# 8-KB slots for all expert weights, with four of them shared in turn with the mixer's normalized input

## The chip, the cores and the metric

The kernel runs on one core of one Trainium2 chip. The metric is the device time of one execution in microseconds (us). The kernel before was timed in three runs: 1904.22, 1905.45 and 1908.49 us, median 1905.45 us. Differences under about 0.2% (3.8 us) can't be told from no change.

## The reference, cut to what matters

Two decoder layers over 512 tokens of 1024 numbers, all in float32. Each layer has a mixer and a mixture of experts (MoE):

```python
for l in range(2):
    sh1, sc1, g1, sh2, sc2, g2 = split(silu(c) @ ada_w[l] + ada_b[l])
    h = rmsnorm(x, norm1_g[l]) * (1 + sc1) + sh1
    x = x + g1 * hybrid_mixer(h, w_in[l], ...)      # three kinds of attention, one output projection
    h = rmsnorm(x, norm2_g[l]) * (1 + sc2) + sh2
    x = x + g2 * hier_moe(h, ...)                   # top 1 of 4 groups, top 2 of 8 experts in it
return rmsnorm(x, final_g)

# one expert:  (silu(xc @ w1[e]) * (xc @ w3[e])) @ w2[e],  w1, w3: 1024x512, w2: 512x1024
```

A layer has 32 experts. Each has 4 MB of first weights (w1 and w3) and 2 MB of second weights (w2), so a layer reads 192 MB of expert weights, once.

## The kernel before, in words

**Mixer.** `ln1` normalizes x, transposes it and keeps it as `h`: eight 4-KB tiles (high and low part of a 128-row block; sizes here are per partition, of which there are 128). `proj_qk` and `proj_v` multiply `h` with the input projection's weights; the last of them is the second half of `proj_qk(1)` ("q1" in the list `ORDER`). After it nothing reads `h`. `ORDER` is written out by hand and interleaves attention units (`sb`, `fox`, `nsa`), projections, conditioning vectors (`ada`), output projection (`p..`, `w..`) and the four `tail` sequences, each of which ends the mixer for 128 tokens and starts their routing: `moe_in` transposes x into `xT` for the router and `moe_parts` writes the normalized rows to DRAM (`rows`, line 1173, issued by ACT).

**MoE.** `route` ranks tokens per expert. `gather` (line 1355, issued by POOL) fetches the rows of two experts at a time by an indirect DMA into `XR`, `turn` transposes them into `xeT`, `up(e)` multiplies with w1 and w3 (line 1380), `act(e)` forms the hidden values, `down(e)` multiplies with w2 (line 1410), `down_out` splits the product into a high and a low part `Yh`, `Yl`, and once for each two experts `scatter` (line 1442) multiplies with a selection matrix and adds to x (line 454). In the source the order is up(e), down(e-1), act(e), scatter for even e.

**Loads.** All weights come by DMAs that SP issues (line 227) in the order of the list `todo`. `pump` gives the next load a free slot. There are two kinds of slots. 8-KB slots (1 MB over 128 partitions): 3 of the `ring`, which lives through the whole kernel and also serves the mixer's weights, 6 (`r0` to `r5`) in the MoE's pool, 2 (`t0`, `t1`) used once at the MoE's start; they hold first weights, four loads an expert. 4-KB slots (512 KB): `s0`, `u0` and eight tiles of the pool tag `L`, of which six stay in use; they hold second weights, four loads an expert. `L` has 18 tiles of 4 KB, which the mixer uses for `h`, the split queries and keys, the values and the output projection's inputs, and the MoE for `xr`, `xeT`, `G`, `Yh` and `Yl`. At the MoE's start `early` issues 18 loads in the order of `FREED`. The pools of mixer and MoE lie over the same memory, so `r`, `t`, `s` and `u` slots are free only when the mixer's tiles under them have been read for the last time.

**Order.** The framework in which the kernel is written orders the instructions of each engine when the kernel is built: an instruction is placed when its inputs and its tile are there by the framework's own account of durations, the earlier one in the source first. The engines then run that order as it stands and wait by semaphores. `keep_in_program_order` pins a few instructions. So the order of `up`, `down` and `scatter` on PE can differ from the source.

Of the kernel before, what the change touches and what calls it, by code (L numbers as in the profile page):

```python
# [10 lines left out]
F32 = mybir.dt.float32  # L11
# [77 lines left out]


RING, RING2, RINGT = 3, 6, 2
BIG = "ring", "r", "t"

FREED = "s0 r0 r2 r1 L L L L r5 t0 t1 u0 r4 r3 L L l l"

PT_K = 0, 1024, 1792, 2304
PT_W = 2560
BUFS = {"L": 18, "v": 1, "W": 8, "P": 4, "o": 6, "us": 4}
ROT = [i ^ 8 if i < 16 else i for i in range(32)]


# [12 lines left out]
class K:  # L114
# [63 lines left out]
    def plan(self):  # L178
        a, t = self.a, self.todo
        for l in self.layers:  # L180
            for s in dict.fromkeys(self.loads(l)):
                if s[0] == "ada":
                    m, nm, c = s[1:4]
                    col = MOD[nm] * 1024 + c * 512
                    for h in range(2):
                        t.append((("ada", m, nm, c, h), a["ada_w"][m, col // 512, h], [128, 4, 512]))
                elif s[0] == "qk":
                    t.append((("wqk", l, s[1]), a["wqk"][l, s[1]], [128, 2, NK, 128]))
                elif s[0] == "v":
                    t.append((("wv", l, s[1]), a["wv"][l, s[1]], [128, NK, 256]))  # L190
                elif s[0] == "cmp":
                    for kv in "kv":
                        t.append((("cmp", l, kv), a["cmp_w1_" + kv][l], [128, 16, 128]))
                elif s[0] == "prep" or s == ("tail", 0):
                    ks = s[1] if s[0] == "prep" else (3,)
                    src = a["w_out"][l, 128 * ks[0]:128 * ks[-1] + 128, :].rearrange("(j p) n -> p j n", p=128)
                    t.append((("wo", l, ks), src, [128, len(ks), D]))
            if self.moe_on:

                for e in range(NE + 1):  # L200
                    for h in range(4 if e < NE else 0):
                        t.append((("w13", l, e, h), a["expert_w13"][l, e, h], [128, 2, 2, 512]))
                    for h in range(4 if e else 0):
                        t.append((("w2", l, e - 1, h), a["expert_w2"][l, e - 1, 128 * h:128 * h + 128, :], [128, D]))

    def pump(self):
        full = set()
        for x in list(self.todo):
            key, src, shape = x
            own = key[0] in ("w13", "w2") and key[1] == self.layer  # L210

            if self.limit and not own or len(full) == 2:
                return
            big = key[0] != "w2"
            slot = next((p for p in self.free if (p.rstrip("0123456789") in BIG) == big and (p == "ring" or own)), None)
            if slot is None:
                full.add(big)
                continue
            if big in full:
                continue  # L220
            self.todo.remove(x)
            self.free.remove(slot)
            self.load(slot, key, src, shape)

    def load(self, slot, key, src, shape):
        x = self.slot(slot, shape, "ring_" + "_".join(map(str, key)))
# [5 lines left out]
    def early(self):  # L232

        self.pump()
        slots = FREED.split()

        l = self.layer
        once = {"t0": ("w13", l, 1, 2), "t1": ("w13", l, 1, 3), "u0": ("w2", l, 0, 3)}
        self.stay = True
        for s in slots:  # L240
            big = s[0] in "rt"
            i = next(i for i, x in enumerate(self.todo) if (x[0] == once[s] if s in once else
                                                            (x[0][0] == "w13") == big and x[0] not in once.values()))
            self.load(s, *self.todo.pop(i))
        self.stay = False

    def slot(self, slot, shape, name):
        pool, n = {"ring": (self.ring, RING), "L": (self.P, BUFS["L"])}.get(slot.replace("l", "L")) or ((self.T if slot[0] in "tu" else self.M), 1)
        return pool.tile(shape, F32, name=name, tag=slot.replace("l", "L"), bufs=n)

    def get(self, *key):
        if key not in self.tiles:
# [2 lines left out]

    def done(self, *key):
        slot = self.tiles.pop(key)[1]
        if slot[0] not in "tlu":
            self.free.append(slot)
        self.pump()  # L260

# [195 lines left out]
    def mixer(self):  # L457
        l = self.layer
        self.h, self.Q, self.Kt, self.V, self.O = None, {}, {}, {}, {}
        ln, lead = self.ln1(l), self.lead(l)  # L460
        do = {"ada": self.ada, "wo": self.half(self.out_proj), "ln": lambda l: next(ln, None), "lead": lambda l, c: next(lead, None), "qk": self.half(self.proj_qk), "v": self.half(self.proj_v), "prep": self.out_prep,
              "cmp": self.compress, "gates": self.gates, "router": self.router, "tail": self.tail, "parts": self.moe_parts}

        for tag in MIX.split():
            if tag == "tab":
                self.tab = self.M.tile([128, R_W], F32, name="tab")
            elif tag == "sm":
                self.sm = self.M.tile([128, SM_W], F32, name="sm")
            else:
                n, b = {"cp": (128, 2), "cpt": (512, 1), "PTs": (PT_W, 1), "W": (512, BUFS["W"]), "P": (D, BUFS["P"]),  # L470
                        "v": (D, 1), "o": (512, BUFS["o"]), "us": (512, BUFS["us"]), "ss": (2, 4), "PT": (512, 2), "ada_s": (512, 1)}[tag]
                self.M.tile([128, n], F32, name="place", tag=tag, bufs=b)
        if l != self.layers[0]:
            self.smalls(l)
            self.rows(l)
        self.tails, self.halves, self.later, self.ready = {}, {}, [], {}
        gens = {u: getattr(self, u)(l) for u in UNITS}
        wait = 0
        for s in self.steps(l):
            if s[0] in UNITS:  # L480
                if wait < 2:
                    wait += 1
                    if wait == 2:
                        self.ada_flush()
                next(gens[s[0]], None)
                continue
            if s == ("qk", 6) and l == self.layers[0]:
                self.late()
            do[s[0]](*s[1:] if s[0] == "ada" else (l,) + s[1:])
            if s[0] == "ada":  # L490
                wait = 0
        self.ada_flush()
# [16 lines left out]
    def ln1(self, l):  # L509
# [1 line left out]
        first = l == self.layers[0]  # L511
        mods = self.mods[l]
        n1 = {}
        self.h = [self.t4("L", [128, 2, 512], F32R, f"h{k}") for k in range(NK)]

        self.stay = True
        self.pump()
# [610 lines left out]

    def moe(self):
        l = self.layer  # L1130
        self.slot("s0", [128, D], "place")
# [5 lines left out]
        with self.tc.tile_pool(name=f"two{l}", bufs=1, reuse_waits="tile") as self.T:  # L1137
            for i in range(RINGT):
                self.slot(f"t{i}", [128, 2, D], "place")
            self.slot("u0", [128, D], "place")  # L1140
            self.early()
            self.gate_rows(l, "g2", self.gb)
            self.route()
# [5 lines left out]
    def moe_in(self, t):  # L1149
# [1 line left out]
        nc, M, sm = self.nc, self.M, self.sm  # L1151
        x = self.x[:, t, :]
        nx = self.t4("L", [128, D], F32, f"nx{t}")
        xt = self.t4("L", [128, NK, 128], F32, "xT")
        for h in range(2):
            p = self.bank(XTP)
            for k in range(4):
# [131 lines left out]
    def experts(self, l):  # L1289
# [23 lines left out]
                    nc.vector.tensor_sub(rest, wt if i == 0 else rest, x)  # L1313

        def onehot(pr):
            G[pr] = self.t4("L", [128, NT, 2, 64], BF, "G")
            nc.vector.tensor_tensor(G[pr], self.rank[:, :, 2 * pr:2 * pr + 2, None].to_broadcast([128, NT, 2, 64]),
                                    self.cf[:, None, None, C_IOTA + 1:C_IOTA + 65].to_broadcast([128, NT, 2, 64]), op=OP.is_equal)

# [81 lines left out]
        def down(e, then=None):  # L1401
# [93 lines left out]
    def overflow(self, l):  # L1495
# [3 lines left out]
        with self.tc.For_i(0, n, 1) as i:  # L1499
# [44 lines left out]
            nc.vector.tensor_mul(hT, s, p3[:, :, 64:128])  # L1544
            p = self.bank("down")
            for k in range(4):
                w = self.slot(f"r{k}", [128, 1, D], "ov_w")
                src = a["expert_w2"][l][ds(e, 1)].rearrange("o (k p) n -> p (o k) n", p=128)
                nc.sync.dma_start(out=w, in_=src[:, k:k + 1, :])
                for b in range(2):  # L1550
                    nc.tensor.matmul(p[64 * b:64 * b + 64, :], hT[:, k, :], w[:, 0, 512 * b:512 * b + 512],
                                     start=k == 0, stop=k == 3, skip_group_check=True, tile_position=(0, 64 * b))
            y = M.tile([128, 512], F32, name="ov_y", tag="F", bufs=2)
            nc.vector.tensor_mul(y, p, self.gb[:, 0, :])
# [26 lines left out]
def layout(i):  # L1581
# [4 lines left out]
    r["expert_w2"] = g["expert_w2"]  # L1586
# [54 lines left out]
```

## Time and profile before

| | us |
|---|---|
| median of 3 runs | 1905.45 |
| profiled execution, its own time | 1901.83 |
| its span, first to last instruction | 1900.0 |
| MoE of the first layer, first `up` to last `down` | 475.2 to 953.3 |
| MoE of the second layer | 1402.4 to 1881 |

PE (matmuls) is busy for 91% of the span, PEld (weight loads into PE, which overlap) 50%, DVE 52%, ACT 35%, POOL 14%. The page cuts the span into 40 slices of 47.5 us; slices 10 to 19 and 30 to 39 are the two MoE stretches. In a busy row a digit is the share of a slice in tenths. "Idle before <- X" names what ended a wait. A window's row gives, for each engine, busy time and the number of instructions, then the granted clock of PE, the DMA engines' busy share and their GB/s.

### The profile page before, as it was taken

How to read it: one execution, taken by the hardware profiler on the slowest of the kernel's cores; microseconds unless marked ns; L12 is line 12 of the kernel's file. 1: busy time of each engine (PE TensorE's matmuls, PEld its weight loads, DVE VectorE, ACT ScalarE, POOL GpSimd, SP SyncE). 2: the span in 40 equal slices, each digit the busy share in tenths (PEclk: the TensorE clock that was granted, in tenths of full speed). 3: DMA queues.
4: the chain of work that ended last, by engine and by line, in shares of the span. 5: the costliest groups of instructions: out<-in, count | busy, mean ns of one | idle time of the engine just before them, and what ended most of it. 6: DMA issues, size and time to landing. Idle time of an engine off the chain costs nothing. (4 is left out here: it accounts for less than half of the span.)

```text
span 1900.0 us, 24314 instructions
## 1 busy us (share of the span) xinstructions
PE 1736.3 (91%) x9110; PEld 946.1 (50%) x9110; DVE 993.7 (52%) x2016; ACT 657.5 (35%) x1525; POOL 261.6 (14%) x207
## 2 busy tenths in 40 slices
PE   6999999896999999999989998889979999999997
PEld 3766755664344343434466765556533434344343
DVE  3475476776344342534467776676635424334345
ACT  3564344344222222222255543443432222222223
POOL 1242212311000000000043321242000000000000
PEclk9999998898999999999999997789979999999998
DMA  8513245125999999999734342011489999999994
GB/s 309 198 67 134 100 156 199 67 98 216 407 413 411 416 416 416 416 415 417 318 142 146 111 144 111 1 67 67 157 357 405 415 405 416 416 416 417 416 417 176
DMA packets 97258, 512.67 MB, mean 270 GB/s; under 512 B 13048, under 2 KB 14328, under 8 KB 54896
## 3 DMA queue, kind: packets, MB, share of 16 engines
q1 hardware_dynamic: 90768, 496.77, 65.5%
q0 software_dynamic: 5216, 10.09, 1.4%
q10 hardware_dynamic: 1152, 4.19, 0.6%
q8 instruction: 75, 1.23, 0.3%
q14 instruction: 47, 0.39, 0.1%
HBM read 512.05 MB, written 6.29 MB: 273 GB/s over the span
## 5 line engine op out<-in xcount | busy, mean ns | idle before, releaser
L1380 PE MATMUL up<-ring_w,xeT 128*64 128x512 f32 x2048 | 488.6, 597 | 0.0
L1380 PEld LDWEIGHTS up<-ring_w,xeT 128*64 128x64 f32 x2048 | 155.9, 138 | 278.6 <-issue 247.7
L1410 PE MATMUL down<-ring_w,hT 128*64 128x512 f32 x1024 | 266.7, 600 | 0.0
L587 PE MATMUL pj<-h,wh 128*128 128x512 f32 x512 | 166.6, 406 | 1.0 <-ACT us L600 1.0
L454 DVE TENSOR_TENSOR x<-x,sc 128x512 f32<-128x512 f32 x256 | 157.7, 683 | 7.6 <-PE sc L1442 6.7
L1399 DVE TENSOR_TENSOR hT<-sil,fT 128x256 f32<-128x256 f32 x64 | 26.7, 417 | 251.5 <-ACT sil L1397 251.2
L1420 DVE TENSOR_TENSOR us<-down,gb 128x512 f32<-128x512 f32 x64 | 44.2, 690 | 205.1 <-PE down L1410 204.4
L1388 ACT ACTIVATE F<-up,small 128x512 f32<-128x512 f32 x64 | 44.0, 688 | 295.5 <-PE up L1380 295.0
L1355 POOL DMA_INDIRECT xr<-rows,index x32 | 31.9, 996 | 788.6 <-PE xg L1364 653.4
L1410 PEld LDWEIGHTS down<-ring_w,hT 128*64 128x64 f32 x1024 | 73.6, 136 | 115.8 <-issue 99.8
L1442 PE MATMUL sc<-Yh,S 128*128 128x512 f32 x256 | 95.6, 438 | 38.3 <-ACT Yh L276 38.3
L276 ACT CAST Yh<-us 64x512 fp32r<-64x512 f32 x128 | 78.5, 613 | 149.6 <-DVE us L1420 140.1
L771 PE MATMUL S<-k,q 64*128 64x512 f32 (+3 forms) x576 | 114.1, 412 | 15.4 <-DVE sbc L999 9.6
L1397 ACT ACTIVATE sil<-fT 128x256 f32<-128x256 f32 x64 | 24.5, 383 | 283.3 <-PE fT L1393 283.2
L798 ACT ACTIVATE Pm<-S,sm_m 128x128 f32<-128x128 f32 (+3 forms) x160 | 83.1, 526 | 85.7 <-DVE sm_m L795 77.0
L587 PEld LDWEIGHTS pj<-h,wh 128*128 128x128 f32 x512 | 96.1, 192 | 24.7 <-ACT us L600 2.6
L587 PE MATMUL pj<-h,wl 128*128 128x512 f32 x256 | 102.5, 402 | 0.0
L277 POOL TENSOR_TENSOR wl<-ring_wqk,wh 128x512 fp32r<-128x512 f32 x56 | 74.4, 1340 | 198.8 <-ACT wh L276 188.1
L1368 ACT ACTIVATE xeT<-xg,mods 128x128 f32<-128x128 f32 x256 | 92.6, 473 | 17.7 <-PE xg L1364 17.6
L1442 PE MATMUL sc<-Yl,S 128*128 128x512 f32 x256 | 91.7, 423 | 0.3 <-DVE Yl L277 0.3
L277 DVE TENSOR_TENSOR Yl<-us,Yh 64x512 fp32r<-64x512 f32 x128 | 87.3, 682 | 8.6 <-ACT Yh L276 6.2
L1442 PEld LDWEIGHTS sc<-Yh,S 128*128 128x128 f32 x256 | 48.9, 201 | 80.0 <-ACT Yh L276 64.5
(332 smaller groups left out, 2719.1 us busy)
## 6 DMA issues: line engine op xcount, KB each, us to landing
ring_w<-in_expert_w SPq DMA_DIRECT2D x256, 1024.0 KB, 11.5
ring_w<-in_expert_w SPq DMA_DIRECT2D x256, 512.0 KB, 14.2
ring_ada_sc<-in_ada_w SPq DMA_DIRECT2D x16, 1024.0 KB, 6.1
ring_ada_sh<-in_ada_w SPq DMA_DIRECT2D x16, 1024.0 KB, 6.3
ring_ada_g<-in_ada_w SPq DMA_DIRECT2D x16, 1024.0 KB, 4.9
ring_wqk<-in_wqk SPq DMA_DIRECT2D x16, 1024.0 KB, 4.8
ring_wv<-in_wv SPq DMA_DIRECT2D x6, 1024.0 KB, 5.4
rows<-nx ACTq DMA_DIRECT2D x8, 512.0 KB, 3.6
```

Source lines behind the costliest of these rows:

```text
L276: (he or self.nc.scalar.copy)(hi, x)
L277: (le or self.nc.vector).tensor_sub(lo, x, hi)
L454: self.nc.vector.tensor_add(x, x, p)
L587: nc.tensor.matmul(p, x[:, k % 4, :], self.h[k][:, y, :], start=k == 0 and i == 0, stop=k == NK - 1 and i == 2)
L771: nc.tensor.matmul(s[:, b, :n], q[r, x, 128 * i:128 * i + 128], k[r, y, :n], start=j == 0, stop=j == 2)
L798: nc.scalar.activation(p[:, j, :n], s[:, j, :n], AF.Exp, bias=m[:, j:j + 1], accum_out=m[:, 2 + j:3 + j])
L1368: nc.scalar.activation(XE[pr][:, k, :], p[:, 128 * i:128 * i + 128], AF.Identity, scale=mods[:, 8 + k:9 + k], bias=mods[:, k:k + 1])
L1380: nc.tensor.matmul(p[64 * b:64 * b + 64, :], XE[pr][:, k, 64 * o:64 * o + 64], w[:, b if o else 1 - b, kk, :], start=k == 0, stop=k == 7, ...
L1388: nc.scalar.activation(F[e], p, AF.Copy, scale=SC[:, e:e + 1])
L1410: nc.tensor.matmul(p[64 * b:64 * b + 64, :], H[e][:, f, :], w[:, 512 * c:512 * c + 512], start=f == 0, stop=f == 3, skip_group_check=True, ...
L1420: nc.vector.tensor_mul(y, p, self.gb[:, o, :])
L1442: nc.tensor.matmul(p, ST[pr][c][:, 128 * t:128 * t + 128], Y[pr][j][:, c, :], start=j == 0, stop=j == 1)
```

## The change

- The tag `L` goes from 18 to 10 tiles of 4 KB. A new tag `B` has four tiles of 8 KB in the same pool. `h` now lives in the four `B` tiles (two row blocks in each).
- After the second half of q1, when `h` has been read for the last time, the four `B` tiles are put on the list of free slots and `pump` is called. They take the first weights of expert 0 then, and serve as ring slots until the MoE's end.
- Second weights are laid out on the host as [layer, expert, 2, 128, 2, 1024] and loaded in two loads of 1 MB with rows of 8192 bytes instead of four of 512 KB with rows of 4096. `down` takes two of its four parts from each and frees the slot after the second.
- All expert loads share one kind of slot: 3 `ring`, 4 `B`, 6 `r`, and `t0`, `t1` once (with expert 0's second weights). `s0` and `u0` are gone, and no `L` tile holds weights. `pump` goes through one list in order.
- `early` issues 8 loads, in the order r0 r2 r1 r5 t0 t1 r4 r3.
- `xT` moves from the tag `L` to the mixer's tag `P` (4 tiles of 4 KB, which the softmax also uses), `G` from `L` to a MoE tag of its own with 3 tiles of 1 KB.
- The loop for experts with more than 64 tokens reads the new layout; it has no iteration here.

```diff
-FREED = "s0 r0 r2 r1 L L L L r5 t0 t1 u0 r4 r3 L L l l"
+FREED = "r0 r2 r1 r5 t0 t1 r4 r3"
-BUFS = {"L": 18, "v": 1, "W": 8, "P": 4, "o": 6, "us": 4}
+BUFS = {"L": 10, "B": 4, "v": 1, "W": 8, "P": 4, "o": 6, "us": 4}
...
-                    for h in range(4 if e else 0):
-                        t.append((("w2", l, e - 1, h), a["expert_w2"][l, e - 1, 128 * h:128 * h + 128, :], [128, D]))
+                    for h in range(2 if e else 0):
+                        t.append((("w2", l, e - 1, h), a["expert_w2"][l, e - 1, h], [128, 2, D]))
...
     def pump(self):
-        full = set()
+        wait = False
         for x in list(self.todo):
             key, src, shape = x
             own = key[0] in ("w13", "w2") and key[1] == self.layer
-            if self.limit and not own or len(full) == 2:
+            if self.limit and not own:
                 return
-            big = key[0] != "w2"
-            slot = next((p for p in self.free if (p.rstrip("0123456789") in BIG) == big and (p == "ring" or own)), None)
+            slot = next((p for p in self.free if (p != "ring" if wait else p == "ring" or own)), None)
             if slot is None:
-                full.add(big)
-                continue
-            if big in full:
-                continue
-            self.todo.remove(x)
-            self.free.remove(slot)
-            self.load(slot, key, src, shape)
+                if own:
+                    return
+                wait = True
+            elif own or not wait:
+                self.todo.remove(x)
+                self.free.remove(slot)
+                self.load(slot, key, src, shape)
...
-        once = {"t0": ("w13", l, 1, 2), "t1": ("w13", l, 1, 3), "u0": ("w2", l, 0, 3)}
+        once = {"t0": ("w2", l, 0, 0), "t1": ("w2", l, 0, 1)}
...
             do[s[0]](*s[1:] if s[0] == "ada" else (l,) + s[1:])
+            if s == ("qk", 1) and self.Q.get((1, 1)) and self.moe_on and "B" not in self.free:
+                self.free += ["B"] * BUFS["B"]
+                self.pump()
...
-        self.h = [self.t4("L", [128, 2, 512], F32R, f"h{k}") for k in range(NK)]
+        hs = [self.P.tile([128, 2, 2, 512], F32R, name=f"h{k}", tag="B", bufs=BUFS["B"]) for k in range(NK // 2)]
+        self.h = [hs[k // 2][:, k % 2] for k in range(NK)]
...
-        xt = self.t4("L", [128, NK, 128], F32, "xT")
+        xt = self.t4("P", [128, NK, 128], F32, "xT")
...
-            G[pr] = self.t4("L", [128, NT, 2, 64], BF, "G")
+            G[pr] = M.tile([128, NT, 2, 64], BF, name="G", tag="G", bufs=3)
...
             for f in range(4):
-                w = self.get("w2", l, e, f)
+                w = self.get("w2", l, e, f // 2)
                 for b in range(2):
                     c = b ^ o
-                    nc.tensor.matmul(p[64 * b:64 * b + 64, :], H[e][:, f, :], w[:, 512 * c:512 * c + 512],
+                    nc.tensor.matmul(p[64 * b:64 * b + 64, :], H[e][:, f, :], w[:, f % 2, 512 * c:512 * c + 512],
                                      start=f == 0, stop=f == 3, skip_group_check=True, tile_position=(0, 64 * b))
-                self.done("w2", l, e, f)
+                if f % 2:
+                    self.done("w2", l, e, f // 2)
```

## Rows read from the trace of the kernel before

**Rows 1.** The page, part 1 (PE's busy time) and part 2 (DMA busy tenths and GB/s in 40 slices).

```profile
PE 1736.3 (91%) x9110; PEld 946.1 (50%) x9110; DVE 993.7 (52%) x2016; ACT 657.5 (35%) x1525; POOL 261.6 (14%) x207
...
DMA  8513245125999999999734342011489999999994
GB/s 309 198 67 134 100 156 199 67 98 216 407 413 411 416 416 416 416 415 417 318 142 146 111 144 111 1 67 67 157 357 405 415 405 416 416 416 417 416 417 176
```

**Rows 2.** Waits between 475 and 950 us, the first layer's MoE: engine and line, what it waited for, us in total, times, longest us.

```profile
PEld sc L1442 <- ACT Yh L276: 28.3, 14, 3.3
PE sc L1442 <- ACT Yh L276: 16.1, 12, 2.4
...
PEld up L1380 <- DMA ring_w<-in_expert_w: 5.4, 19, 0.3
PEld down L1410 <- DMA ring_w<-in_expert_w: 5.3, 19, 0.3
```

**Rows 3.** Windows, each from the first `up` of an even expert to that of the next even one: experts 2, 4, 10 (then 11) and 28. Columns as told above.

```profile
497.60:528.40 30.80, 30.80 (x137) 12.21 (x136) 13.66 (x30) 7.22 (x17) 0.99 (x1) 1.00 0.99 396
528.40:558.50 30.10, 29.49 (x139) 12.08 (x139) 16.80 (x39) 6.36 (x14) 0.99 (x1) 1.00 1.02 417
...
620.90:651.10 30.20, 28.42 (x137) 11.84 (x135) 12.38 (x25) 7.00 (x16) 0.99 (x1) 1.00 1.02 416
...
892.40:921.40 29.00, 27.82 (x132) 11.69 (x130) 11.19 (x21) 7.24 (x17) 0.00 (x0) 1.00 1.02 418
```

**Rows 4.** Timeline of PE around two of the first scatters: start us, us, engine, line, operation, how many.

```profile
510.64 1.93 PE L1380 MATMUL up<-ring_w,xeT 128*64 128x512 f32 x6
512.50 0.73 PE L1442 MATMUL sc<-Yh,S 128*128 128x512 f32 x2
...
539.81 2.79 PE L1380 MATMUL up<-ring_w,xeT 128*64 128x512 f32 x10
542.53 0.73 PE L1442 MATMUL sc<-Yh,S 128*128 128x512 f32 x2
```

**Rows 5.** The same around later scatters.

```profile
628.19 2.74 PE L1410 MATMUL down<-ring_w,hT 128*64 128x512 f32 x12
...
631.45 5.79 PE L1380 MATMUL up<-ring_w,xeT 128*64 128x512 f32 x25
636.66 0.64 PE L1410 MATMUL down<-ring_w,hT 128*64 128x512 f32 x1
...
640.63 1.67 PE L1442 MATMUL sc<-Yh,S 128*128 128x512 f32 x6 [1.18 <-ACT Yh L276]
...
670.83 0.96 PE L1442 MATMUL sc<-Yh,S 128*128 128x512 f32 x3 [1.17 <-ACT Yh L276]
```

**Rows 6.** Timeline at the start of the MoE, first and second layer: the first gather and PE's first instruction on its rows.

```profile
465.29 1.07 POOL L1355 DMA_INDIRECT xr<-rows,index  x1 [3.38 <-DVE index L1327]
...
473.23 1.94 PE L1364 MATMUL xg<-cf,xr 128*128 128x128 f32 x8 [7.85 <-DMA xr<-rows,index]
...
1391.37 1.08 POOL L1355 DMA_INDIRECT xr<-rows,index  x1 [25.52 <-DMA ring_w<-in_expert_w]
...
1400.37 1.94 PE L1364 MATMUL xg<-cf,xr 128*128 128x128 f32 x8 [8.84 <-DMA xr<-rows,index]
```

**Rows 7.** From issue to landing: first the 32 gathers of line 1355, then the 8 row writes of line 1173 (512 KB each).

```profile
DMA to landing us min/median/max: 7.1/8.4/10.2
...
DMA to landing us min/median/max: 2.6/3.6/5.6
```

**Rows 8.** Windows inside the two gathers: no PE work in the first, DMA share and GB/s at the end of the row.

```profile
466.00:470.00 4.00, 0.00 (x0) 0.00 (x0) 3.24 (x13) 0.07 (x1) 1.38 (x2) 0.50 1.00 421
...
1391.00:1395.00 4.00, 0.27 (x4) 0.18 (x4) 3.18 (x17) 0.32 (x2) 2.08 (x2) 0.50 1.02 422
```

**Rows 9.** SP: weight loads issued from 460.9 to 471 us and from 1388.2 to 1398 us (start, us from the first to the last issue, how many), then its waits for the row writes from 330 to 480 and from 1260 to 1400 us (us in total, times, longest).

```profile
460.70 8.87 SPq L227 DMA_DIRECT2D ring_w<-in_expert_w  x11
...
1388.33 8.41 SPq L227 DMA_DIRECT2D ring_w<-in_expert_w  x10
...
SPq L227 <- DMA rows<-nx: 33.3, 4, 12.8
...
SPq L227 <- DMA rows<-nx: 24.6, 3, 13.1
```

**Rows 10.** Timeline, first layer: the last `xT` is written by ACT, and PE's matmuls on the last two.

```profile
451.65 0.56 ACT L1159 COPY xT<-pj 128x512 f32<-128x512 f32 x1
...
452.26 3.76 PE L1166 MATMUL pjl<-sm,xT 128*128 128x36 f32 x32
```

**Rows 11.** The last projection that reads `h` in the first layer (durations in ns, first and last start in us), then windows that begin where it ends in the first and in the second layer.

```profile
L587 PE MATMUL pj<-h,wl x16: 390/393/483, 257.5 to 277.0; 128*128 128x512 f32 x16
...
276.50:290.00 13.50, 11.47 (x60) 6.89 (x60) 9.25 (x21) 5.51 (x18) 1.78 (x1) 0.75 0.00 0
1221.40:1235.00 13.60, 7.25 (x42) 3.83 (x40) 12.51 (x14) 7.91 (x16) 8.65 (x5) 0.73 0.00 0
```

**Rows 12.** The DMA view from 500 to 900 us: packets, and the weight loads by size with the median us to landing.

```profile
DMA packets 31343, 165.63 MB, mean 414 GB/s; under 512 B 4271, under 2 KB 4271, under 8 KB 18011
...
ring_w<-in_expert_w SPq DMA_DIRECT2D x107, 1024.0 KB, 12.0
ring_w<-in_expert_w SPq DMA_DIRECT2D x102, 512.0 KB, 14.2
```

More of the change, by code (lines that the diff above doesn't have):

```diff
@@ L91 @@
 RING, RING2, RINGT = 3, 6, 2
-BIG = "ring", "r", "t"
-FREED = "s0 r0 r2 r1 L L L L r5 t0 t1 u0 r4 r3 L L l l"
+FREED = "r0 r2 r1 r5 t0 t1 r4 r3"
 PT_K = 0, 1024, 1792, 2304
 PT_W = 2560
-BUFS = {"L": 18, "v": 1, "W": 8, "P": 4, "o": 6, "us": 4}
+BUFS = {"L": 10, "B": 4, "v": 1, "W": 8, "P": 4, "o": 6, "us": 4}
 ROT = [i ^ 8 if i < 16 else i for i in range(32)]
@@ L237, in early @@
         l = self.layer
-        once = {"t0": ("w13", l, 1, 2), "t1": ("w13", l, 1, 3), "u0": ("w2", l, 0, 3)}
+        once = {"t0": ("w2", l, 0, 0), "t1": ("w2", l, 0, 1)}
         self.stay = True
         for s in slots:
-            big = s[0] in "rt"
-            i = next(i for i, x in enumerate(self.todo) if (x[0] == once[s] if s in once else
-                                                            (x[0][0] == "w13") == big and x[0] not in once.values()))
+            i = next(i for i, x in enumerate(self.todo) if (x[0] == once[s] if s in once else x[0] not in once.values()))
             self.load(s, *self.todo.pop(i))
@@ L247, in slot @@
     def slot(self, slot, shape, name):
-        pool, n = {"ring": (self.ring, RING), "L": (self.P, BUFS["L"])}.get(slot.replace("l", "L")) or ((self.T if slot[0] in "tu" else self.M), 1)
-        return pool.tile(shape, F32, name=name, tag=slot.replace("l", "L"), bufs=n)
+        pool, n = {"ring": (self.ring, RING), "B": (self.P, BUFS["B"])}.get(slot) or ((self.T if slot[0] == "t" else self.M), 1)
+        return pool.tile(shape, F32, name=name, tag=slot, bufs=n)
     def get(self, *key):
@@ L257, in done @@
         slot = self.tiles.pop(key)[1]
-        if slot[0] not in "tlu":
+        if slot[0] != "t":
             self.free.append(slot)
@@ L1130, in moe @@
         l = self.layer
-        self.slot("s0", [128, D], "place")
         for i in range(RING2):
@@ L1139, in moe @@
                 self.slot(f"t{i}", [128, 2, D], "place")
-            self.slot("u0", [128, D], "place")
             self.early()
@@ L1546, in overflow @@
             for k in range(4):
-                w = self.slot(f"r{k}", [128, 1, D], "ov_w")
-                src = a["expert_w2"][l][ds(e, 1)].rearrange("o (k p) n -> p (o k) n", p=128)
-                nc.sync.dma_start(out=w, in_=src[:, k:k + 1, :])
+                if k % 2 == 0:
+                    w = self.slot(f"r{4 + k // 2}", [128, 2, D], "ov_w")
+                    nc.sync.dma_start(out=w, in_=a["expert_w2"][l][ds(e, 1), k // 2].rearrange("o p k n -> p (o k) n"))
                 for b in range(2):
-                    nc.tensor.matmul(p[64 * b:64 * b + 64, :], hT[:, k, :], w[:, 0, 512 * b:512 * b + 512],
+                    nc.tensor.matmul(p[64 * b:64 * b + 64, :], hT[:, k, :], w[:, k % 2, 512 * b:512 * b + 512],
                                      start=k == 0, stop=k == 3, skip_group_check=True, tile_position=(0, 64 * b))
@@ L1585, in layout @@
     r = {"x": g["x"].reshape(S, D), "c": np.ascontiguousarray(g["c"].reshape(NK, 128).T), "cf": cf, "tab": tab, "cb": cb}
-    r["expert_w2"] = g["expert_w2"]
+    r["expert_w2"] = np.ascontiguousarray(g["expert_w2"].reshape(L, NE, 2, 2, 128, D).transpose(0, 1, 2, 4, 3, 5))
     for n in ("cmp_w1_k", "cmp_w1_v"):
```

## The prediction

> **What bounds the kernel now.** I read the page first. PE is busy for 91% of the span, and the DMA row shows two plateaus at nine tenths and some 415 GB/s, which are the two MoE stretches [rows 1]. Two resources that look full at once: the next view must say which of them waits for the other. The waits of the first MoE answer it. PE waited for a weight load 19 times before `up` and 19 before `down`, and never longer than 0.3 us, which is the gap between any two of these weight loads. It waited for `Yh` before the scatter, up to 3.3 us at a time [rows 2]. So the loads keep pace, and the stretch is as long as PE's own order makes it.
>
> Third view: windows of one pair of experts. The early pairs take 30.80 and 30.10 us, with PE busy for 30.80 and 29.49 of them. Later ones take 30.20 with 28.42 busy, so 1.78 us a pair are idle; the last ones, which have no more rows to locate, take 29.00 with 1.18 idle [rows 3]. The timelines say why. Early, some 6 or 10 `up` pieces of the next expert stand between the end of `down` and the scatter, and `Yh` is made behind them [rows 4]. Later `down` is cut in two: twelve pieces, then 25 of `up`, then the last four mixed into the end of `up`, and the scatter right behind them finds no `Yh` [rows 5]. These last four need the fourth quarter of w2. That is the trace of a shortage in the plan: seven 4-KB slots are left after the start, so this quarter can be loaded only when the expert before has begun its `down`.
>
> Fourth view: the start of the MoE. PE stands for 7.85 and 8.84 us until the first gather has landed [rows 6].
>
> Durations are of the profiled execution, 1901.83 us (span 1900.0), which is 3.62 below the median of 1905.45. I make the sum against 1901.83 and move the result up by 3.62.
>
> **The change part by part.**
>
> *Fewer loads beside the first gather.* All 32 gathers take 7.1 to 10.2 us to land, and the queue is full in nearly all; the 512-KB row writes, some of which meet an idle queue, take 2.6 to 5.6 [rows 7]. In both gathers of the start the DMA engines run at full share and 421 and 422 GB/s [rows 8]. What they compete with is a burst of 11 and 10 loads that SP issues at 460.70 and 1388.33. They come so late because the `L` tiles in `FREED` must wait for the row writes, 33.3 and 24.6 us of SP's time, with `r5`, `t0`, `t1`, `r4`, `r3` queued behind them [rows 9]. The change takes the `L` loads out. Five loads of 1 MB are left, 5.24 MB or 12.6 us at 417 GB/s, where the old burst of some 7.9 MB takes 19. They get a new wait: `r5` and `r4` now lie over the `P` tiles, and these hold `xT`, last read at 452.26 + 3.76 = 456.0 [rows 10]. So they run from about 456 to 469, and the gather, issued at 465.3, has its second half for itself. Bounds: with an idle queue it lands 1.1 + 2.6 = 3.7 us after its issue, not 7.9 and 9.0, which gives 4.2 + 5.3 = 9.5 us; at worst it takes the 10.2 of the slowest one, 2.3 and 1.2 us more. I take half of the contention, 2 us a layer: **-4 us**. Next late is `xeT`, 1.1 us behind the gather as now.
>
> *The order of PE inside the pairs.* With one list and 13 slots a load can go out when the piece 13 places ahead is used, 13/6 of an expert or 33 us (six pieces, 15.1 us an expert) before its own use, and w2 has no shortage of its own. I expect the early order to hold through the stretch. What that is worth: from one early scatter to the next it is 542.53 - 512.50 = 30.03 us, and in it four more `up` pieces ran than a pair has (ten against six before the scatter), at 0.21 us each, so 29.2 [rows 4]; late it is 670.83 - 640.63 = 30.20 [rows 5]. That is 1.0 us a pair. The windows say less: 30.10 against 30.20, or even 30.80 [rows 3]. Bounds: all 1.78 us idle gone, or 0.6 us lost. I take 0.6 us gained for nine pairs a layer (12 waits for `Yh` [rows 2], less the three last pairs): 2 x 9 x 0.6 = **-11 us**.
>
> *Loads of w2 in 8192-byte rows.* The count of w2 loads falls from 256 to 128, and the smaller ones now take longer to land than the larger, 14.2 against 12.0 us [rows 12], because they queue. Cost or gain now: nothing, since PE doesn't wait for loads. The cover is what must be checked, as PE gets faster. Weights come at 6.29 MB an expert; at 417 GB/s a pair takes 30.2 us, as long as PE's pair now. If PE's pair falls to 29.5, it gains 0.7 us a pair on the loads, 10 us over a layer; the 13 MB of slots hold 33 us of PE's work. That is enough once, and nothing is left beyond it.
>
> *`B` slots filled early.* `h` is read for the last time at 277 and 1221 us, and in the 13.5 us behind that the queue moves nothing, 0 GB/s [rows 11]. The 4 MB (10 us) lie there at no cost. SP issues four loads that wait for PE's last projection; behind them stand `w_out` and `ada` loads. If one of these were late by those 10 us, some of it would show; I set 0, up to +4.
>
> *`L` with 10 tiles, `xT` in `P`, `G` on its own.* While `h` lives, the rest of `L` is 10 tiles before and after. Behind it 10 are left for four queries, two keys, one gate tile and pairs of inputs to the output projection, and these come in turn. `xT` takes one of four `P` tiles beside two softmax tiles. 0, from -2 to +8. ACT, DVE and POOL do the same instructions as before.
>
> Sum: 1901.83 - 4 - 11 = 1886.8; at the median's place **1890 us**.
>
> **A rule of the skill.** The Trainium skill, "DMA: Bandwidth & Descriptors", section "Anatomy of one DMA", gives a DMA a fixed 2.0 us and bytes over 436 GB/s. By it four w2 loads would cost 12.8 us and two 8.8 us, an estimate of 4 us less an expert, and a queue that is paid load by load would be the bound. The trace has 165.63 MB in 400 us with both sizes mixed, 414 GB/s, so the fixed part is hidden behind the other loads in flight [rows 12]. By the rule the MoE would lose all its idle time; this is the fourth rival below.
>
> **The rivals.**
>
> *The order stays as it is or the loads bind:* only the gather's 4 us come. For it: the DMA row is full, 30.2 us a pair is the same for both, and a plan that thinks its queue full may cut `down` again. Against it: the waits show no load that was late. 1905.45 - 4 = 1901.5 us.
>
> *The later block makes a longer stall (slower):* the second half of `down`, eight pieces instead of four, is placed behind `up` when the plan has the second 1-MB block arrive after `up`'s end. Then `Yh` starts later, and every scatter waits as long as the longest did, 3.3 us, where the mean of PEld's 14 waits is 28.3 / 14 = 2.0 [rows 2]. Price 1.3 us for 18 pairs, +23, with the gather's 4 off: 1905.45 + 23 - 4 = 1924 us. It decides from the point at which that block lands, in the plan, later than the last `up` piece; the 33 us speak against it.
>
> *Scratch too tight (slower):* softmax tiles wait for `xT` in `P`, or the output projection's inputs for `L`, and the mixers lose 4 us each, while the pairs gain nothing beyond the gather: 1905.45 + 8 - 4 = 1909.5 us.
>
> *All idle gone:* 1.78 us in each of 18 pairs, -32, and -4: 1869 us. Against it: even the early pairs aren't that short.
>
> **How the numbers follow.** Chances: forecast 0.45, order as it is 0.25, longer stall 0.12, scratch 0.08, all idle gone 0.10. About 0.2%, 3.8 us, is what this kernel's timing can tell from no change, so faster begins below 1901.6 and slower above 1909.3. Faster: 0.41 of the forecast's 0.45, half of the second case, all of the last, 0.64. Same: the other half of the second, a little of the first and of the scratch case, 0.17. Slower: 0.19. The range 1876 to 1908 leaves out most of the two slow cases and of the fastest, about 0.2. The forecast's own range is 1880 to 1899.
>
> **What would show it.** Right: the gap before the first `xg` at some 5 to 6 us in place of 7.85 and 8.84; `up` pieces between `down` and each scatter, with no wait for `Yh` over 1 us; pairs near 29.6 us; SP's waits for `rows<-nx` gone. Wrong: four or eight `down` pieces in front of the scatter; waits of PE for `ring_w` over 0.3 us, which would mean that the loads bind; new waits in the mixer before `Pm` or `oh`.

## The result, and the profile after

The changed kernel takes 1925.03 us (median of 4 runs, 1920.40 to 1925.95), the kernel before 1904.84 (4 runs): ratio 1.011, 95% interval 1.0079 to 1.0141. It is slower by 20 us, where the forecast was 15 us faster. The profiled execution took 1920.40 us, its span is 1918.5. The page, in answer to [rows 1]:

```profile
PE 1764.8 (92%) x9110; PEld 935.6 (49%) x9110; DVE 992.7 (52%) x2016; ACT 664.0 (35%) x1525; POOL 263.1 (14%) x207
...
DMA  8413355124899999999634243211389999999992
GB/s 321 180 66 133 113 228 197 67 89 188 345 412 420 419 418 418 416 419 420 265 132 154 99 153 112 88 66 66 143 326 397 413 413 418 419 419 418 419 415 84
```

The DMA row is as full as before, and the number of matmuls is the same, but PE is busy for 28.5 us more. Cut at the first gather, the first `up` and the last `down` of each layer, the two traces differ in the MoE above all (us; each cut is the start of an instruction, the last `down` that of its last weight load into PE, 1.0 us before `down` ends):

| | before | after | |
|---|---|---|---|
| start to first gather | 465.3 | 468.5 | +3.2 |
| first gather to first `up` | 9.9 | 10.3 | +0.4 |
| first layer, first `up` to last `down` | 477.1 | 485.7 | +8.6 |
| last `down` to the second layer's first gather | 439.1 | 436.0 | -3.1 |
| first gather to first `up` | 11.0 | 10.6 | -0.4 |
| second layer, first `up` to last `down` | 477.7 | 485.4 | +7.7 |
| last `down` to the end | 19.9 | 22.0 | +2.1 |

Windows of two pairs of the changed kernel (same columns as [rows 3]):

```profile
608.70:639.40 30.70, 29.47 (x135) 11.70 (x136) 12.45 (x25) 7.50 (x16) 0.98 (x1) 1.00 1.02 420
639.40:670.10 30.70, 29.47 (x135) 11.68 (x136) 12.42 (x25) 7.50 (x16) 0.98 (x1) 1.00 1.01 419
```

From one scatter to the next it is 30.73 us in place of 30.20, with 1.23 idle in place of 1.78 and 29.47 busy in place of 28.42. From one first `up` to that of the next pair, the last three full pairs take 30.5 against 29.0, and the first one 23.8 against 22.4 (in the second layer 23.5 against 23.0). Against that, two pairs in each MoE of the kernel before took 32.6 and 32.2, with the granted clock at 0.95 in them (558.5 to 591.1 and 711.9 to 744.1 us), and none of the regular pairs of the changed one did.

Do the loads bind now? First the waits on them in the whole span, then those before the scatter from 475 to 950 us ([rows 2]):

```profile
PEld up L1380 <- DMA ring_w<-in_expert_w: 5.4, 19, 0.3
PEld down L1410 <- DMA ring_w<-in_expert_w: 4.1, 22, 0.4
```

```profile
PEld sc L1443 <- ACT Yh L273: 30.4, 15, 2.1
...
PE sc L1443 <- ACT Yh L273: 17.2, 14, 1.2
```

They do not: no wait for a load is longer than 0.4 us. An estimate from the times of the DMA packets and landings: a block of weights lies there 16 to 22 us before its first use, from the fourth pair to the last. This time is called the lead below. In the kernel before, the last quarter of an expert's w2 had a lead of some 11 us in the early pairs and 2 in the last ones, the other blocks more, at least some 16 and at the end 7. What is left is PE's order. The timeline of one pair, in answer to [rows 5]:

```profile
669.98 0.73 PE L1443 MATMUL sc<-Yh,S 128*128 128x512 f32 x2 [1.23 <-ACT Yh L273]
...
674.01 5.36 PE L1380 MATMUL up<-ring_w,xeT 128*64 128x512 f32 x22
679.31 0.77 PE L1364 MATMUL xg<-cf,xr 128*128 128x128 f32 x5
680.00 1.94 PE L1380 MATMUL up<-ring_w,xeT 128*64 128x512 f32 x8
681.87 0.55 PE L1364 MATMUL xg<-cf,xr 128*128 128x128 f32 x3
682.35 1.94 PE L1410 MATMUL down<-ring_w,hT 128*64 128x512 f32 x8
...
685.65 1.94 PE L1410 MATMUL down<-ring_w,hT 128*64 128x512 f32 x8
687.42 7.04 PE L1380 MATMUL up<-ring_w,xeT 128*64 128x512 f32 x32
694.28 1.89 PE L1410 MATMUL down<-ring_w,hT 128*64 128x512 f32 x8
696.10 0.66 PE L1393 MATMUL fT<-cf,F 128*128 128x128 f32 x4
696.69 1.94 PE L1410 MATMUL down<-ring_w,hT 128*64 128x512 f32 x8
698.46 1.02 PE L1380 MATMUL up<-ring_w,xeT 128*64 128x512 f32 x2
700.71 0.73 PE L1443 MATMUL sc<-Yh,S 128*128 128x512 f32 x2 [1.23 <-ACT Yh L273]
```

`down` is cut in eight and eight, in every expert from the fourth to the last but one. The second eight end at 698.6, two pieces of `up` follow, and the scatter waits for `Yh` until 700.71. Before, five pieces of `up` stood in that gap:

```profile
668.15 0.59 PE L1410 MATMUL down<-ring_w,hT 128*64 128x512 f32 x1
668.20 1.45 PE L1380 MATMUL up<-ring_w,xeT 128*64 128x512 f32 x5
```

A piece is one record of PE, and a matmul of the source on 64 of the 128 columns (the 128*64 of the row) makes two of them. So the two pieces now in the gap are one such matmul, whose partner on the other 64 columns runs alone behind the scatter; the section on the forecast has its price.

### The profile page after: what moved, and what is told of

It is laid out like the page before. It is cut to its first block, busy times and chain, and to the rows that moved or that the text cites. A ratio compares the mean times of both kernels' runs of the same rounds, so it can differ in the third digit from the quotient of the medians.

```text
span 1918.5 us, 24132 instructions
## 1 busy us (share of the span) xinstructions
PE 1764.8 (92%) x9110; PEld 935.6 (49%) x9110; DVE 992.7 (52%) x2016; ACT 664.0 (35%) x1525; POOL 263.1 (14%) x207
## 3 DMA queue, kind: packets, MB, share of 16 engines
q8 instruction: 75, 1.23, 0.3%
## 5 line engine op out<-in xcount | busy, mean ns | idle before, releaser
L1380 PE MATMUL up<-ring_w,xeT 128*64 128x512 f32 x2048 | 497.3, 600 | 0.0
L1380 PEld LDWEIGHTS up<-ring_w,xeT 128*64 128x64 f32 x2048 | 150.5, 138 | 292.2 <-issue 282.3
L1410 PE MATMUL down<-ring_w,hT 128*64 128x512 f32 x1024 | 246.4, 601 | 0.0
L1435 DVE TENSOR_SCALAR S<-sb,cf 128x512 fp32r<-128x512 f32 x64 | 47.4, 747 | 247.6 <-PE sb L1433 247.5
L1443 PE MATMUL sc<-Yh,S 128*128 128x512 f32 x256 | 102.0, 419 | 42.7 <-ACT Yh L273 37.4
L1410 PEld LDWEIGHTS down<-ring_w,hT 128*64 128x64 f32 x1024 | 66.0, 136 | 108.3 <-issue 102.6
L274 DVE TENSOR_TENSOR Yl<-us,Yh 64x512 fp32r<-64x512 f32 x128 | 87.8, 686 | 33.9 <-ACT Yh L273 30.5
L1443 PE MATMUL sc<-Yl,S 128*128 128x512 f32 x256 | 101.2, 416 | 0.1
L773 PEld LDWEIGHTS S<-k,q 64*128 64x128 f32 x576 | 56.1, 201 | 66.2 <-issue 36.8
L840 PE MATMUL T<-cf,Pm 128*128 128x128 f32 x400 | 72.5, 311 | 14.3 <-DVE PTs L270 8.1
```

Of the source, the lines that this page charges most:

```text
L274: (le or self.nc.vector).tensor_sub(lo, x, hi)
L773: nc.tensor.matmul(s[:, b, :n], q[r, x, 128 * i:128 * i + 128], k[r, y, :n], start=j == 0, stop=j == 2)
L840: self.nc.tensor.transpose(t[:, kt - k, b], p[:, b, 128 * kt:128 * kt + 128], self.ident)
L1380: nc.tensor.matmul(p[64 * b:64 * b + 64, :], XE[pr][:, k, 64 * o:64 * o + 64], w[:, b if o else 1 - b, kk, :], start=k == 0, stop=k == 7, ...
L1435: nc.vector.tensor_scalar(s, p, self.cf[:, C_PM:C_PM + 1], None, op0=OP.is_equal)
L1443: nc.tensor.matmul(p, ST[pr][c][:, 128 * t:128 * t + 128], Y[pr][j][:, c, :], start=j == 0, stop=j == 1)
```

## The experiments

Theory A: what the changed kernel pays is PE's order, which the build makes. Theory B: a pair loads 12 blocks of 1 MB and its tokens' rows, 12.9 MB, which at 419 GB/s are 30.7 us, so the loads set the pair. The first four kernels below tell these apart:

**e1, the changed kernel with a fixed order.** The source emits the instructions in the wanted order, and each PE instruction of the experts is tied behind the one emitted before it (cut):

```diff
                 self.done("w13", l, e, h)
+                if h == 2 - 1 and e % 2 and e >= 3:
+                    scatter(e // 2 - 1)
...
-            if e >= 2 and e % 2 == 0:
-                scatter(e // 2 - 1)
-            elif e > 1:
+            if e > 1 and e % 2:
                 places(e // 2)
+            if e >= 4:
+                self.pin(mark)
...
+        for x, y in zip(pe[k - 1:], pe[k:]):
+            self.tc.add_manual_dep(y, x.name, mybir.DependencyInfo(mybir.DependencyClass.NoSync, mybir.DependencyReason.DATA),
+                                   reason="pin")
```

> The changed kernel with PE's order in the experts fixed by hand: per pair all 16 down pieces of an expert in one block, then 16 up pieces, then the scatter; loads and slots untouched. Theory A (order): the MoE got slower because the build placed the second half of down and the up pieces by its own account of when loads arrive. In the changed kernel weights land 16 to 22 us before their use. By counts a pair then needs 96 x 0.2146 + 4.0 + 1.2 + 1.2 + 0.7 + 0.2 + 5 x 0.15 = 28.6 us in place of 30.72, no wait for Yh, until the 17 us in hand are used up (2.1 us a pair, 8 pairs); so some 17 us a layer less, 1925 - 34 = 1891 us, and waits of PE for ring_w in the last pairs. Theory B (loads): 12.9 MB a pair at 419 GB/s are 30.7 us, just the pair's time, so the loads set it already: 1925 us, pairs of 30.7, the idle time moves from Yh to ring_w from the first pairs on.

Measured: 1883.44 us (4 runs), ratio to the kernel before 0.9918 (0.9891 to 0.9944). Its timeline, then two early and two late windows:

```profile
563.52 7.09 PE L1380 MATMUL up<-ring_w,xeT 128*64 128x512 f32 x32
570.54 0.26 PE L1324 MATMUL wc<-pieces,G 128*128 128x8 bf16 x4
570.72 3.65 PE L1412 MATMUL down<-ring_w,hT 128*64 128x512 f32 x16
574.31 0.66 PE L1395 MATMUL fT<-cf,F 128*128 128x128 f32 x4
574.89 3.65 PE L1380 MATMUL up<-ring_w,xeT 128*64 128x512 f32 x16
578.48 0.50 PE L1445 MATMUL sc<-Yh,S 128*128 128x512 f32 x1
...
582.40 3.65 PE L1380 MATMUL up<-ring_w,xeT 128*64 128x512 f32 x16
585.99 1.09 PE L1364 MATMUL xg<-cf,xr 128*128 128x128 f32 x8
587.01 3.23 PE L1412 MATMUL down<-ring_w,hT 128*64 128x512 f32 x14
```

```profile
561.50:589.90 28.40, 28.40 (x136) 11.53 (x134) 12.56 (x24) 7.16 (x16) 0.99 (x1) 1.00 1.01 420
589.90:618.20 28.30, 28.30 (x136) 11.54 (x134) 12.56 (x24) 7.16 (x16) 0.98 (x1) 1.00 1.02 420
790.00:820.50 30.50, 29.01 (x136) 11.41 (x134) 11.87 (x23) 7.09 (x17) 0.98 (x1) 1.00 1.01 420
850.00:880.50 30.50, 28.91 (x132) 11.37 (x130) 11.42 (x20) 7.14 (x17) 0.44 (x1) 1.00 1.01 420
```

Theory A, in both halves, and 8 us more than the 34 expected. A pair takes 28.32 us with PE never idle, for seven pairs; by then the lead is used up, and the last pairs take 30.5 us at 420 GB/s, which is the pace of the loads. 41.6 us came from the order of the same instructions.

**e2, the kernel before with the same order.** The same edit in before.

> The kernel before with the same fixed order of PE. Theory A: in the kernel before the loads' lead over PE shrinks from some 25 us at the MoE's start to 1 to 2 us at its end, so a faster order of PE finds the loads in its way: at most 2 to 4 us a layer less, 1898 to 1902 us, and PE waits for ring_w in the second half. Rival (order alone bounds both kernels): pairs of 28.6 us, 1.6 us less for 13 pairs a layer, 1905 - 42 = 1863 us.

Measured: 1907.24 us (10 runs), ratio 1.0031 (1.0015 to 1.0048): no gain, even 4 us lost, where theory A had 3 to 7 gained. The MoEs take 478.5 and 477.3 us, as before. Two of its pairs, then its waits from 475 to 960 us:

```profile
672.90:702.10 29.20, 26.48 (x121) 9.36 (x121) 9.36 (x19) 7.28 (x16) 0.98 (x1) 0.94 1.02 417
702.10:734.70 32.60, 30.71 (x145) 13.18 (x144) 14.49 (x28) 7.28 (x16) 0.99 (x1) 1.00 1.02 416
```

```profile
PEld down L1412 <- DMA ring_w<-in_expert_w: 41.0, 47, 3.6
...
PE down L1412 <- DMA ring_w<-in_expert_w: 20.4, 12, 2.7
...
PEld up L1380 <- DMA ring_w<-in_expert_w: 6.9, 21, 0.6
```

The idle time has moved from `Yh` to the loads, and nearly all of it to those of w2. So the kernel before had nothing to gain from this order, since its loads could not feed it, and the change did give room: 1907.24 - 1883.44 = 23.8 us under the same order of PE.

**e3, the changed kernel with another place for w2 in the list of loads.** No order is fixed:

```diff
                 for e in range(NE + 1):
-                    for h in range(4 if e < NE else 0):
-                        t.append((("w13", l, e, h), a["expert_w13"][l, e, h], [128, 2, 2, 512]))
-                    for h in range(2 if e else 0):
-                        t.append((("w2", l, e - 1, h), a["expert_w2"][l, e - 1, h], [128, 2, D]))
+                    for h in range(5):
+                        if h == (2 if e > 1 else 4):
+                            for f in range(2 if e else 0):
+                                t.append((("w2", l, e - 1, f), a["expert_w2"][l, e - 1, f], [128, 2, D]))
+                        if h < 4 and e < NE:
+                            t.append((("w13", l, e, h), a["expert_w13"][l, e, h], [128, 2, 2, 512]))
```

> The changed kernel with one edit in the list of loads: the two w2 loads of an expert stand between the second and the third w13 load of the next expert, not behind the fourth. No order is fixed by hand. Built so, PE's order becomes scatter, 16 up, xg, 16 down and 16 up, fT, sb, 8 up, wc, 8 up and 16 down and 16 up, fT. Theory A: the order follows the list through the build's account of arrivals, and this one has 16 up pieces (3.4 us) and the fT between down and the scatter, so no wait for Yh: within 5 us of e1. Theory B: 1925 us as e1.

Measured: 1895.97 us (10 runs), ratio 0.997 (0.9951 to 0.9989): 29 us under the changed kernel, but 12.5 above e1, not within 5. The order came out as expected and the wait for `Yh` is gone. A new one stands in its place, twice a pair, since `fT` now comes straight behind the last `up` pieces (pairs of 29.81 us):

```profile
617.47 3.60 PE L1382 MATMUL up<-ring_w,xeT 128*64 128x512 f32 x16
621.92 0.66 PE L1395 MATMUL fT<-cf,F 128*128 128x128 f32 x4 [0.85 <-ACT F L1390]
```

A list of loads thus sets the order of PE, though on the chip PE waits for none of them.

**e4, e1 with w2 in 4096-byte rows.** Each w2 load becomes two of 512 KB, into the same slots:

```diff
-        load = self.nc.sync.dma_start(out=x, in_=src)
+        for j in range(2 if key[0] == "w2" else 1):
+            load = self.nc.sync.dma_start(out=x[:, j, :], in_=src[:, j, :]) if key[0] == "w2" else self.nc.sync.dma_start(out=x, in_=src)
```

> e1 with each w2 load split in two of 512 KB whose rows are 4096 bytes, into the same slots, in the same order of PE. A packet of 4096 bytes takes 163 ns in the trace of before, one of 8192 takes 314, so a pair's loads take 8 x 314 + 8 x 163 in place of 12 x 314 (ratio 1.0127): 31.1 us in place of 30.7. If the loads bind in e1 (theory A, second half; theory B, all of it), this is 3 to 6 us a layer slower than e1, 6 to 12 us in all. If rows of 8192 bytes are worth nothing, the same as e1 within 3 us.

Measured: 1892.54 us (9 runs), 9.1 more than e1, within the 6 to 12. The seven pairs before the loads bind take 28.32 us in both, the later ones 30.8 in place of 30.5. So fewer loads with longer rows (the run changes both together) are worth 9 us where the loads bind and nothing where they don't.

Then the start of the MoE and the early fill.

**e5 and e9, e1 without the early fill.** The `B` slots come onto the free list where the MoE starts:

```diff
-            if s == ("qk", 1) and self.Q.get((1, 1)) and self.moe_on and "B" not in self.free:
+            if s == ("qk", 1) and self.Q.get((1, 1)) and self.moe_on and False:
...
     def early(self):
...
+        self.free += ["B"] * BUFS["B"]
+        self.stay = True
         self.pump()
```

The line with `stay`, which keeps SP's loads in the order of the source, is e9's alone.

> e1 without the early fill: the four B slots come onto the free list where the MoE starts, not behind q1. If the loads bind in e1 from the middle of each MoE on, 4 MB that are loaded some 190 us later cost their own time, 4 x 2.5 us = 10 us a layer: 1883 + 20 = 1903 us. Rival (the fill is worth nothing, since loads lead anyway): 1883 us.

Measured: 1884.50 us (4 runs). But its four loads still went out at 271 us: the build had moved them back, and e5 says nothing of the fill. So again with the loads held in order:

> e5 again, with SP kept from issuing the loads into B ahead of the mixer's other loads (in e5 the build moved them back to 271 us, so that e5 had the early fill after all). Now expert 0's loads go into the ring from 370 us on and the B slots are filled around 425 us. Theory from e5's trace: the queue has room there, all these loads land before the burst at 461 us, and the fill at q1 is worth nothing: 1883 us, within 4. Rival (4 MB less lead cost 10 us a layer, because the loads bind at the end): 1903 us.

Measured: 1884.23 us (4 runs), against 1883.44. The fill behind q1 is worth nothing here: the queue has room for those 4 MB later.

**e6 and e7, five early loads held back** until the first gather has landed, in the changed kernel and in e1:

```diff
             if pr < 2:
-                gather(pr)
+                g = gather(pr)
+                if pr == 0:
+                    self.early(g.ins)
...
+            if after is not None and s == slots[3]:
+                x = [x for x in self.nc.cur_bb.bb.instructions[first:] if x.engine == mybir.EngineType.SP][-1]
+                self.tc.add_manual_dep(x, after.name, mybir.DependencyInfo(mybir.DependencyClass.Sync, mybir.DependencyReason.DATA), reason="hold")
```

The second call of `early` issues r5, t0, t1, r4 and r3, and r5's load waits for the gather.

> The changed kernel, PE's order as built, with the last five early loads (r5 t0 t1 r4 r3) made to wait for the first gather. If the gather's 8.2 us come from the loads in front of it, it lands 4 to 5 us after its issue and PE's first wait is some 4 us shorter, in each layer; the loads go out 11 us later, which the 17 us by which weights lead PE here still cover: 1925 - 8 = 1917 us. Rival (8 us is the gather's own time): 1925 us.

> The same hold of five loads in e1, where the loads bind at the MoE's end and nothing covers them. The gather gains its 4 us a layer at the start, and the end is set by loads that run some 8 to 11 us later: 1883 + 16 to 22 = 1899 to 1905 us. Rival (PE's order still sets e1): 1883 - 8 = 1875 us.

Measured: e6 1914.45 us (9 runs), 10.6 under the changed kernel; e7 1888.94 (4 runs), 5.5 above e1. First the changed kernel's wait for the two first gathers, then that of e6 and of e7 (each: us in total, times, longest):

```profile
PE xg L1364 <- DMA xr<-rows,index: 16.7, 2, 8.4
```

```profile
PE xg L1369 <- DMA xr<-rows,index: 7.8, 2, 4.3
```

```profile
PE xg L1369 <- DMA xr<-rows,index: 7.8, 2, 4.2
```

So the loads in front of the gather cost 4.5 us a layer. In e7 nothing covers the later loads, and it is slower, in the direction told but by 5.5 us, not by 16 to 22. Its MoEs are 8.7 and 7.5 us longer than e1's (473.1 and 471.4 against 464.4 and 464.0), 16 in all, but the two waits for the gathers are 8.9 us shorter, and I had not taken that gain off.

**e8, e1 with `xT` back in the tag `L`:**

```diff
-        xt = self.t4("P", [128, NK, 128], F32, "xT")
+        xt = self.t4("L", [128, NK, 128], F32, "xT")
```

> e1 with xT back in the tag L, which keeps its 10 tiles. In the changed kernel SP waited 30.6 us for the last xT, from 427.8 to 461.7 us, before r5's load and the four behind it. Without xT in P these five wait only for the softmax tiles, whose last reads lie around 445 us. Theory: the five loads (12.5 us) run before the gather, which then lands in 4 to 5 us, and all later loads come 10 to 12 us earlier, up to 12 us a layer: 1860 to 1870 us. Rival (something else under r5 is as late, or the tails wait for an L tile): 1883 us or some us more.

Measured: 1874.16 us (4 runs), ratio 0.9837 (0.9807 to 0.9868): 9.3 less than e1, not 13 to 23. The waits of SP from 400 to 500 us, first of the changed kernel, then of e8, and e8's waits for the gathers:

```profile
SPq L226 <- DVE xT L1159: 30.6, 1, 30.6
...
SPq L226 <- PE pjl L1166: 2.7, 1, 2.7
```

```profile
SPq L226 <- PE T L788: 21.7, 1, 21.7
SPq L226 <- DMA rows<-nx: 13.8, 3, 8.4
```

```profile
PE xg L1364 <- DMA xr<-rows,index: 7.5, 2, 4.1
```

The five loads go out between 451 and 466 us, in e1 between 466 and 468, and the last of them has landed about when the gather is issued at 470.84; its rows are there 3.5 us later. The waits for the two gathers are 9.2 us shorter than in e1 (7.5 against 16.7), which is the whole gain. The MoE itself is as long (465.1 us, in e1 464.4): the load behind the five goes out at 479.3, when PE has freed a slot. e8 is the fastest kernel of this study, 1.6% under the kernel before.

**e10, `down` cut as built, but the scatter later.** Is it the cut of `down` or the bare wait for `Yh`?

```diff
-                if f == 0 and then is not None:
+                if f == (0 if then == NE - 1 else 1) and then is not None:
                     act(then)
+                    if then % 2 and then < NE - 1:
+                        places(then // 2)
...
-                if h == 2 - 1 and e % 2 and e >= 3:
+                if h == 3 - 1 and e % 2 and e >= 3:
```

This diff is against e1. `fT` now stands between the halves of `down`, and the scatter behind 24 pieces of `up`.

> The changed kernel with a fixed order of PE that keeps what the build did to down (the two halves apart, fT between them, the second one in front of or behind a whole up) and changes one thing: 24 up pieces, not 2, stand between the end of down and the scatter. If what the changed kernel pays is the wait for Yh with nothing behind it (2.15 us from the end of down to the scatter in its trace), a pair falls by 2.2 us to some 28.4 us until the loads bind, as in e1: 1883 us, within 4. Rival (the cut of down itself costs, by more stretches on half of the array): a pair of 30 us and more, above 1900 us.

Measured: 1880.03 us (4 runs), ratio 0.9891 (0.9861 to 0.992). The timeline around the scatter, and a window:

```profile
597.29 1.94 PE L1412 MATMUL down<-ring_w,hT 128*64 128x512 f32 x8
599.16 0.66 PE L1395 MATMUL fT<-cf,F 128*128 128x128 f32 x4
599.75 1.94 PE L1412 MATMUL down<-ring_w,hT 128*64 128x512 f32 x8
601.51 5.32 PE L1380 MATMUL up<-ring_w,xeT 128*64 128x512 f32 x24
```

```profile
590.00:618.40 28.40, 28.40 (x136) 11.53 (x134) 12.63 (x26) 7.39 (x16) 0.99 (x1) 1.00 1.02 421
```

The cut of `down` is free. What counts is what stands between its end and the scatter: enough of `up`, and no matmul without its partner. This run changes both and does not tell them apart.

## Why the prediction was wrong

**The step that failed** is "The order of PE inside the pairs". It read the cut of `down` in [rows 5] as "the trace of a shortage in the plan", of seven 4-KB slots, and concluded that with one list "w2 has no shortage of its own" and "the early order" would "hold through the stretch". On the chip the shortage was there (e2's waits are nearly all for w2), and the slots did become enough: weights led PE by 16 to 22 us. But the order is made before the chip runs, and it did not become the early one: with w2 behind the four w13 loads of the list, `down` stayed cut from the fourth expert on; with w2 in the middle (e3) it was whole in every expert. What arrival times the build reckons with stands in no trace, so that it takes the loads for slower than they are is argued from the orders alone, not shown. In place of -11 us came +16.3, 8.6 and 7.7 in the two MoEs. One of the prediction's own signs of being wrong came with it: eight `down` pieces in front of the scatter.

The first section of the prediction had already gone half wrong: "the stretch is as long as PE's own order makes it". With 2 us of lead left at the end, and nothing gained from another order in e2, the loads were as near a bound as PE was.

**The price, in a pair.** e1 gives the unit: 32 pieces of `up` take 570.54 - 563.52 = 7.02 us and 16 take 3.59, so a piece costs 0.214 and a stretch of them 0.16 more. By this the changed kernel's 22 pieces should take 4.87 and take 679.31 - 674.01 = 5.30, and its two pieces before the scatter should take 0.59 and take 1.02: 0.43 more in each case, the time of the missing partner. With the 1.23 idle, 0.15 for `xg` in two parts and 0.11 for a slower scatter that is 2.35 of the 2.40 us between 30.72 and e1's 28.32. In the kernel before, 1.78 of the 1.88 us above 28.32 are idle. So the change traded 0.55 us of idle time for 0.86 of half-used array and 0.2 of work cut into smaller parts. That a lone piece costs as much as two is read from these rows; e10 took the wait and the lone piece away together and doesn't separate them. The Trainium skill, "TensorEngine Tiling (Array Packing)", section "Key Properties", says that different tiles of the array can run matmuls in parallel; the trace agrees: pieces on the two halves start 6 ns apart, and 0.43 us is lost when one has no partner.

**The rival that came true** is "The later block makes a longer stall", with 1924 us forecast for it and 1925.03 measured. Its place was right: eight pieces of `down` behind `up`, in front of the scatter. Its price of 1.3 us for 18 pairs was not: the idle time is shorter than before, and the 0.52 us a regular pair and 1.5 in each of the last three came as shown above. Also, the -4 for the gather in its sum measured 0. That the totals lie 1 us apart is luck. It got a chance of 0.12, because "the 33 us speak against it": a lead on the chip was held against an order that is fixed before the chip runs.

**The gather, -4 us:** measured 0; the two waits come to 16.7 us in both kernels, and "from about 456 to 469" fails; this is the second step that failed. The step took the last read of `xT` from the timetable of before, 456.0. In the changed kernel that read ends at 461.64 and the loads go out from 461.72 on, right before the gather at 468.51. The mechanism itself was right, and even its upper bound of 9.5 us for both layers: e6 and e8 gained 8.9 and 9.2 us on these waits. The move of `xT` into `P`, costed at nothing, is what kept this from showing.

**Rows of 8192 bytes, 0:** right, for the reason given, and so is the reckoning of 30.2 us a pair at the loads' pace (30.5 in e1). e4 adds what they are worth, with the smaller number of loads, once the loads bind: 9.1 us.

The prediction weighed a rule (the Trainium skill, "DMA: Bandwidth & Descriptors", section "Anatomy of one DMA"), which that section gives for DMAs that GpSimd issues, while SP issues these loads. Carried over to them, its 2.0 us for each of e4's 128 more loads would be 256 us in all, an estimate, if they were paid one by one. The 9.1 us measured say that here, with several loads in flight, it is not paid load by load, also where the loads bind.

**`B` filled early, 0:** right (e9). **`L`, `xT` and `G`, 0:** the mixers moved by +3.2 and -3.1 us; apart from `xT`'s part in the gather it holds.

**"All idle gone", 1869 us:** with the order fixed and `xT` in `L` the kernel reaches 1874, with nearly all idle time before the scatter gone. The sentence against it, "even the early pairs aren't that short", was true of the kernel before but no bound: 28.3 us are possible. **"The loads bind":** not in this kernel, but they are the next bound, seven pairs into e1.

## What to carry to other kernels

Where a build-time scheduler orders an engine, find out from the built order and not from the chip's slack what it believes: a change of buffers or of the list of loads is a change of that order, and it can cost more than the loads give. To see what a layout is worth, fix the engine's order by hand in both kernels first; here the same change was worth -24 us under a fixed order and +20 without. And when a tile moves into memory that a load will reuse, its last read becomes that load's start: look who is queued behind.

## Unexpected

A gather of 128 rows takes 3.5 us from issue to its rows in e8, where the loads in front of it have landed, and over 8 us in the changed kernel, beside five loads of 1 MB. Loads that are merely placed later in the source went out at the same time (e5): only an order that is held makes such an experiment. The pieces on 64 columns cost 0.214 us each when both halves of the array are in use and 0.43 alone, so an odd number of such matmuls before a break is worth avoiding.
